# Scaling the weights of a Strassen-like FFN before they are split, and a third accumulator bank

## The chip, the cores and the metric

The kernel runs on one core of one Trainium2 chip. The metric is the device time of one execution in microseconds (us), the median of several runs. The core has a matmul engine (TensorE, PE in the profile, with its weight loads shown apart as PEld), and VectorE (DVE), ScalarE (ACT), GpSimd (POOL) and SyncE (SP, which here only issues transfers). Every engine takes its own queue of instructions strictly in order; semaphores tie the queues to each other.

## The reference

A transformer block on a sequence of 1024 tokens of width 1024: a first FFN, a mixer with two attentions, a second FFN, a final norm. What matters here are the two FFNs:

```
h = rmsnorm(x, ffn_norm)            # (x * rsqrt(mean(x^2) + eps)) * gain
x = x + 0.5 * ((silu(h @ w1) * (h @ w3)) @ w2)     # w1, w3: 1024 x 2816; w2: 2816 x 1024
```

All inputs are fp32. The changed code is the up-projection, `h @ w1` and `h @ w3`, of both FFNs.

## The kernel before

Activations are held transposed: eight tiles of 128 features by 512 tokens for each half of the tokens (tb 0 and 1). The 2816 columns of w1 and w3 are 22 groups f of 128; one weight tile in DRAM, `w13[f, j]`, holds half j of the 1024 rows for one group, w1 and w3 side by side (128 x 1024 values, 512 KB).

*Precision.* A product in fp32 accuracy is made from halves: a tile is split into a high and a low part, and three matmuls (high·high, high·low, low·high) are added up in a PSUM bank. In the first two pairs of groups of an FFN ("plain" blocks, `NPLAIN = 2`) the halves are fp32r. In the other nine pairs (fp = 2 to 10) they are fp16, and to fit the range of fp16 weights and activations are first multiplied by a power of two: `hs` for the activations (from the norm's gains), and one scale per block for the weights. `find_scale` (L342) takes it from the sums of squares of the block's four raw weight tiles: four ACT squares (L340), a matmul with ones that adds them over the partitions (L344, output `tot`), then seven small DVE instructions (L346, L102 to L111). The second output, `inv`, undoes both scales and is applied where PSUM is read.

`split16` (L93 to L95) makes the fp16 halves: ACT writes `scale * src` as fp16, and DVE writes `scale * src - high` as fp16, with a scalar_tensor_tensor. `form` (L317) does this for one weight tile into the next of eight slots.

*A block.* Instead of eight products of 2 x 2 sub-blocks a block of two column groups takes seven (a Strassen-Winograd scheme). The raw tiles are a11, a21, a22, a12; four sums of them are made in place or in `s1`, `s4` (L425 to L428), by POOL, in the first block by DVE:

```
se.tensor_tensor(out=s1, in0=a21, in1=a22, op=ALU.add)          # L425: S1
se.tensor_tensor(out=a21, in0=a11, in1=a21, op=ALU.subtract)    # L426: S3
se.tensor_tensor(out=a11, in0=s1, in1=a11, op=ALU.subtract)     # L427: S2
se.tensor_tensor(out=s4, in0=a12, in1=a11, op=ALU.subtract)     # L428: S4
```

The activations' sub-blocks B11, B21, B22 and sums T1 to T4 are split once, ahead of the blocks (`scale_h`, `right_sums`). Each product is 24 matmuls (two banks m = 0, 1 for w1 and w3, four tiles, three terms), all on line L397. In the order of the code they are: A11·B11 into X (`first_product`, written at the end of the block before, right after that block's `find_scale` call for the next block); S2·T2 into Y; S1·T1 into Z; A12·B21 on top of X; S3·T3 on top of Y; then, after the next block's scale and its A11·B11, A22·T4 on top of Y and S4·B22 into Z. Between them the partial sums are read: ACT copies X after A11·B11 (L407, `s`), DVE adds Y and `s` after S2, S3 and A22 (L433: outputs u for S2 and S3, c for A22), adds Z (L455 after S1, L469 after S4), and L442, L443 finish the first output. SiLU and the gate follow (L510 on ACT, L511 on POOL), and the results and four sums of them (L479, POOL) go to DRAM for the down-projection. Between, DVE also makes sums of the w2 tiles (L499 to L505) for it.

X, Y and Z have two PSUM banks each, and the same two in every block. One bank is for `tot`; one of the eight is not used. Raw tiles are double-buffered, so the next block's tiles are loaded and squared during a block.

*What sets the order.* The code is not run in the order in which it is written. A planner fixes each engine's queue before the run: it goes through an assumed timeline, and gives each engine the earliest written instruction whose inputs it takes to be ready at that moment. An instruction can thus be put ahead of earlier written ones that still wait. At run time the queues are not changed any more. A few instructions are moved by a priority offset (`high_priority`) or a fixed order (`order_after`).

Of the kernel before, what the change touches and what calls it, by code (L numbers as in the profile page):

```python
# [7 lines left out]
F32 = mybir.dt.float32  # L8
# [4 lines left out]
AF = mybir.ActivationFunctionType  # L13
ALU = mybir.AluOpType
# [4 lines left out]
P = 128  # L19
T = 1024  # L20
TB = 512
# [3 lines left out]
KD = 8  # L25
# [64 lines left out]
    return lo_of(nc, lo, src, hi)  # L90


def split16(nc, t, src, scale):  # L93
    nc.scalar.activation(out=t[:, 0], in_=src, func=AF.Copy, scale=scale)  # L94
    return nc.vector.scalar_tensor_tensor(out=t[:, 1], in0=src, scalar=scale, in1=t[:, 0], op0=ALU.mult, op1=ALU.subtract)  # L95


def pow2_scale(K, pool, tot, shift, other=None):
# [16 lines left out]
def gain_scales(K, pool):  # L115
    nc = K.nc
    sq = pool.tile([P, 4, KD], F32, tag="gsq", name="gsq")
    nc.vector.tensor_tensor(out=sq, in0=K.gain, in1=K.gain, op=ALU.mult)
    r = pool.tile([P, 4], F32, tag="gr", name="gr")
    nc.vector.tensor_reduce(out=r, in_=sq, axis=AX.X, op=ALU.add)  # L120
    tot = K.pt.tile([P, TB], F32, tag="acc", name="tot")[:, 0:4]
    nc.tensor.matmul(tot, lhsT=K.ones, rhs=r, start=True, stop=True)
    K.hs, K.hinv = pow2_scale(K, pool, tot, 57)


def load_w(K, src):
# [110 lines left out]
def scale_h(K, tb, gi, gates=None):  # L237
    nc = K.nc
    K.h[tb], last = [None] * KD, []
    hs = K.hs[:, gi:gi + 1]  # L240
    for k in [i // 2 + i % 2 * (KD // 2) for i in range(KD)] if gates else range(KD):
        x = K.x[tb][k]
        g = K.gain[:, gi, k:k + 1]
        if gates:
            order_after(K, nc.scalar.activation(out=x, in_=x, func=AF.Copy, scale=g), gates[k])
            nc.gpsimd.tensor_tensor(out=x, in0=x, in1=K.R[tb], op=ALU.mult)
        else:
            nc.vector.scalar_tensor_tensor(out=x, in0=x, scalar=g, in1=K.R[tb], op0=ALU.mult, op1=ALU.mult)
        if gates:
            K.h[0][k] = K.hp.tile([P, 2, TB], F16, tag=f"hi0_{k}", name="h16")  # L250
            split16(nc, K.h[0][k], x, hs)
            continue
        hi = K.hp.tile([P, TB], F32R, tag=f"hi{tb}_{k}", name="hi")
        lo = K.hp.tile([P, TB], F32R, tag=f"lo{tb}_{k}", name="lo")
        last.append(split(nc, hi, lo, x))
        K.h[tb][k] = hi, lo
    if gates:
        K.b22 = []
        for k in range(KD // 2):
            K.b22.append(K.hp.tile([P, 2, TB], F16, tag=f"lo0_{k}", name="h16"))  # L260
            split16(nc, K.b22[k], K.x[1][k + KD // 2], hs)
    return last


# [6 lines left out]
    return x  # L271


def right_sums(K, tp, gi):
    nc = K.nc
    h = KD // 2
    T = [[], [], [], []]

    def put(i, k, src):
        t = (tp if i else K.hp).tile([P, 2, TB], F16, tag=f"t{i}_{k}" if i else f"lo0_{k + h}", name="tf")  # L280
        split16(nc, t, src, K.hs[:, gi:gi + 1])
        T[i].append(t)
    for k in range(h):
        b11, b21, b12, b22 = K.x[0][k], K.x[0][k + h], K.x[1][k], K.x[1][k + h]
        nc.vector.tensor_tensor(out=b11, in0=b12, in1=b11, op=ALU.subtract)
        put(0, k, b11)
        nc.gpsimd.tensor_tensor(out=b12, in0=b22, in1=b12, op=ALU.subtract)
        put(2, k, b12)
        nc.vector.tensor_tensor(out=b22, in0=b22, in1=b11, op=ALU.subtract)
        put(1, k, b22)  # L290
        nc.gpsimd.tensor_tensor(out=b21, in0=b21, in1=b22, op=ALU.subtract)
        put(3, k, b21)
    return T

# [14 lines left out]
def ffn_up(K, w13, w2, ctx0, gi, first):  # L309
    nc = K.nc  # L310
    h = KD // 2
    ctx = ExitStack()
# [1 line left out]
    bank = lambda n, m: ps.tile([P, TB], F32, tag=f"{n}{m}", name=n)  # L314
    K.nw = 0

    def form(src, sc):  # L317
        n = len(K.wpools)
        t = K.wpools[K.nw % n].tile([P, 2, KD, P], F16, tag=("whi", "wlo")[K.nw // n % 2], name="w16")
        K.nw += 1  # L320
        split16(nc, t.rearrange("p a k c -> p a (k c)"), src.rearrange("p k c -> p (k c)"), sc)
        return t

    def store(f, tb, t):
# [24 lines left out]
    with ExitStack() as c1:  # L349
# [5 lines left out]
        r = load(NPLAIN)  # L355
        nu = 0
        for tb, p in ((0, 0), (0, 1), (1, 1), (1, 0)):
            for f in range(2):
                nu += 1
                u = [bank("XYZ"[nu % 3], m) for m in range(2)]  # L360
                for m in range(2):
                    for k in range(KD):
                        mm3(nc, u[m], ws[p][2 * f + k // h], m * h + k % h, K.h[tb][k], k == 0, k == KD - 1)
                t = sb.tile([P, TB], F32, tag="s", name="s")
                if tb == 0:
                    nc.vector.tensor_tensor(out=t, in0=u[0], in1=K.R[0], op=ALU.mult)
                    order_after(K, nc.scalar.activation(out=t, in_=t, func=AF.Silu), K.rdone)
                    nc.gpsimd.tensor_tensor(out=t, in0=t, in1=K.R[0], op=ALU.mult)
                else:
                    nc.scalar.activation(out=t, in_=u[0], func=AF.Silu)  # L370
                nc.vector.tensor_tensor(out=t, in0=u[1], in1=t, op=ALU.mult)
                store(2 * p + f, tb, t)
            if (tb, p) == (0, 0):
                gates = scale_h(K, 1, gi)
            if (tb, p) == (0, 1):
                scale_h(K, 0, gi, gates)
                for i in range(4):
                    square(r, i)
                scale, inv = find_scale(r, K.pt)
    K.nw = 0  # L380
    T = right_sums(K, open_pool(K, ctx, "tf", 1, side="right"), gi)
    ctx0.close()
    with ctx:
        pt = open_pool(K, ctx, "up_tot", 1, True)
        sums = open_pool(K, ctx, "up_sums", 1)
        rw.append(open_pool(K, ctx, "up_raw2", 1))
        po = open_pool(K, ctx, "up_post", 1)
# [9 lines left out]
                    K.mark = nc.tensor.matmul(o, lhsT=w[:, a, m * h + k], rhs=x[k][:, b], start=start and k == 0 and i == 0,  # L397
                                              stop=k == h - 1 and i == 2, skip_group_check=True)

        def first_product(a11, sc, inv):  # L400
            X = [bank("X", m) for m in range(2)]
            w = form(a11, sc)
            s = []
            for m in range(2):
                prod(X[m], w, m, B11, True)
# [2 lines left out]
            return X, s  # L408

        n0, n1 = NPLAIN, NF // 2  # L410
        X, sv = first_product(r[0][0], scale, inv)
        for fp in range(n0, n1):
            f0, f1 = 2 * fp, 2 * fp + 1
            a11, a21, a22, a12 = r[0]
# [4 lines left out]
            for n in ("u2", "u3", "c21", "c11"):  # L419
                for m in range(2):  # L420
                    if n != "c11" or m == 0:
                        u[n, m] = po.tile([P, TB], F32, tag=f"{n}{m}", name=n)
            Y, Z = [[bank(n, m) for m in range(2)] for n in "YZ"]
            se = nc.vector if fp == n0 else nc.gpsimd
            se.tensor_tensor(out=s1, in0=a21, in1=a22, op=ALU.add)  # L425
            se.tensor_tensor(out=a21, in0=a11, in1=a21, op=ALU.subtract)  # L426
            se.tensor_tensor(out=a11, in0=s1, in1=a11, op=ALU.subtract)  # L427
            se.tensor_tensor(out=s4, in0=a12, in1=a11, op=ALU.subtract)  # L428
            ws2, ws1, wa12, ws3 = [form(t, scale) for t in (a11, s1, a12, a21)]

            def add(n, o, i, inv):
                for m in range(2):
# [21 lines left out]
            for m in range(2):  # L454
                nc.vector.scalar_tensor_tensor(out=u["u3", m], in0=Z[m], scalar=inv, in1=u["u3", m], op0=ALU.mult, op1=ALU.add)  # L455
            finish_a(K, u["u3", 0], u["u3", 1], f1, 1, store)
            wa22, ws4 = form(a22, scale), form(s4, scale)
            old = inv
            if fp + 1 < n1:
                scale, inv = find_scale(r, pt)  # L460
                X, nxt = first_product(r[0][0], scale, inv)
            for m in range(2):
                prod(Y[m], wa22, m, T[3], False)
            add("c21", Y, sv, old)
# [1177 lines left out]
```

## Time and profile before

| | us |
|---|---|
| median of 3 runs | 2987.51 (2986.30 to 2988.24) |
| the profiled execution | 2990.17 |
| its span, first to last instruction | 2988.4 |
| seven-product blocks of FFN 1, about | 104 to 467 |
| seven-product blocks of FFN 2, about | 2403 to 2761 |

The granted TensorE clock is 0.986 of full speed. In a row of the profile `L95 DVE SCALAR_TENSOR_TENSOR w<-a,sc,w` is line 95, the engine, the operation, the output and the inputs by their names in the code; durations follow in ns or, in a timeline, start and length in us; a bracket `[0.82 <-DVE w L95]` is the engine's idle time ahead of the instruction and what ended it. In a wait table, `PE Y L397 <- DVE u L433: 29.0, 15, 3.2` says that PE waited 29.0 us in 15 places, 3.2 at the longest, with a matmul into Y, for line 433 on DVE. A stretch's row gives its length and then each engine's busy time and number of instructions.

### The profile page before, as it was taken

How to read it: one execution, taken by the hardware profiler on the slowest of the kernel's cores; microseconds unless marked ns; L12 is line 12 of the kernel's file. 1: busy time of each engine (PE TensorE's matmuls, PEld its weight loads, DVE VectorE, ACT ScalarE, POOL GpSimd, SP SyncE). 2: the span in 40 equal slices, each digit the busy share in tenths (PEclk: the TensorE clock that was granted, in tenths of full speed). 3: DMA queues.
4: the chain of work that ended last, by engine and by line, in shares of the span. 5: the costliest groups of instructions: out<-in, count | busy, mean ns of one | idle time of the engine just before them, and what ended most of it. 6: DMA issues, size and time to landing. Idle time of an engine off the chain costs nothing. (4 is left out here: it accounts for less than half of the span.)

```text
span 2988.4 us, 40209 instructions
## 1 busy us (share of the span) xinstructions
PE 2835.6 (95%) x14276; PEld 2128.7 (71%) x14276; DVE 1995.5 (67%) x3282; ACT 1370.2 (46%) x2347; POOL 951.9 (32%) x765
## 2 busy tenths in 40 slices
PE   8998999999999899989899999999999998999998
PEld 6543447888788688778788888888878853444886
DVE  7866566666587467667777777776333966665656
ACT  7434334443333145445566666666432644432443
POOL 3348441000145123322333333333242436554101
PEclk9999999999999999999999999999999999999999
DMA  4354447655456544544332235222743246444854
GB/s 159 117 194 170 178 155 267 214 189 163 147 200 230 184 142 169 186 157 163 127 117 86 82 115 161 79 83 77 289 152 109 77 149 208 173 151 157 298 183 148
DMA packets 212712, 478.21 MB, mean 160 GB/s; under 512 B 20896, under 2 KB 39584, under 8 KB 212512
## 3 DMA queue, kind: packets, MB, share of 16 engines
q1 hardware_dynamic: 212512, 475.65, 46.2%
q8 instruction: 112, 1.84, 0.3%
q14 instruction: 88, 0.72, 0.1%
HBM read 313.56 MB, written 162.00 MB: 159 GB/s over the span
## 5 line engine op out<-in xcount | busy, mean ns | idle before, releaser
L397 PEld LDWEIGHTS <-w 128*128 128x128 f16 x3024 | 298.4, 99 | 414.4 <-issue 45.9
L52 PE MATMUL gm<-hi,whi 128*128 128x512 f32 x880 | 352.1, 400 | 3.3 <-ACT whi L89 1.9
L397 PE MATMUL Y<-tf,w 128*128 128x512 f16 x1296 | 304.2, 389 | 48.0 <-DVE u L433 29.0
L54 PE MATMUL gm<-hi,wlo 128*128 128x512 f32 x880 | 348.4, 397 | 0.3 <-DVE wlo L85 0.3
L53 PE MATMUL gm<-lo,whi 128*128 128x512 f32 x880 | 348.3, 396 | 0.0
L861 PE MATMUL S<-kt,qt 128*128 128x320 f32 (+5 forms) x1152 | 274.9, 352 | 36.4 <-ACT Pt L870 12.2
L85 DVE TENSOR_TENSOR tl<-tr,th 128x512 fp32r<-128x512 f32 (+2 forms) x384 | 236.2, 619 | 88.3 <-ACT th L89 85.0
L89 ACT ACTIVATE th<-tr 128x512 fp32r<-128x512 f32 (+2 forms) x384 | 203.8, 542 | 198.2 <-PE tr L916 194.7
L85 DVE TENSOR_TENSOR wlo<-st,whi 128x1024 fp32r<-128x1024 f32 x154 | 197.4, 1299 | 112.6 <-ACT whi L89 111.5
L868 DVE CUSTOM_DVE_ANT_0 S<-S,slab 128x896 f32<-128x896 f32 (+7 forms) x320 | 224.4, 708 | 65.5 <-PE S L861 59.5
L53 PE MATMUL acc<-wlo,whi 128*128 128x512 f32 (+1 forms) x628 | 243.1, 387 | 1.0 <-DVE wlo L85 1.0
L54 PE MATMUL acc<-whi,wlo 128*128 128x512 f32 (+1 forms) x628 | 242.1, 388 | 0.0
L89 ACT ACTIVATE whi<-st 128x1024 fp32r<-128x1024 f32 x154 | 160.6, 1057 | 177.2 <-PE acc L54 107.4
L52 PE MATMUL acc<-whi 128*128 128x512 f32 (+1 forms) x628 | 240.4, 387 | 0.0
L1027 POOL TENSOR_SCALAR Ps<-Ps,l 128x384 f32<-128x384 f32 (+7 forms) x128 | 100.8, 787 | 425.0 <-DVE l L1025 216.4
L861 PEld LDWEIGHTS S<-kt,qt 128*128 128x128 f32 x1152 | 183.4, 190 | 61.0 <-ACT Pt L870 14.2
L397 PE MATMUL X<-h,w 128*128 128x512 f16 x864 | 195.1, 379 | 0.0
L52 PEld LDWEIGHTS gm<-hi,whi 128*128 128x128 f32 x880 | 168.5, 191 | 36.3 <-ACT whi L89 2.1
L54 PEld LDWEIGHTS gm<-hi,wlo 128*128 128x128 f32 x880 | 168.1, 191 | 36.8 <-DVE wlo L85 0.9
L95 DVE SCALAR_TENSOR_TENSOR w<-a,sc,w 128x1024 f16<-128x1024 f32 x90 | 180.3, 2019 | 18.8 <-ACT w L94 17.4
L53 PEld LDWEIGHTS gm<-lo,whi 128*128 128x128 f32 x880 | 168.6, 192 | 30.8
L85 DVE TENSOR_TENSOR wlo<-wst,whi 128x1024 fp32r<-128x1024 f32 x103 | 137.0, 1332 | 44.1 <-ACT whi L89 32.9
(320 smaller groups left out, 6260.8 us busy)
## 6 DMA issues: line engine op xcount, KB each, us to landing
wst<-in_win_dram SPq DMA_DIRECT2D x55, 512.0 KB
sw<-w2s SPq DMA_DIRECT2D x44, 512.0 KB
st<-sw SPq DMA_DIRECT2D x88, 256.0 KB
st<-saT SPq DMA_DIRECT2D x88, 256.0 KB
a<-in_f1w_dram SPq DMA_DIRECT2D x36, 512.0 KB
a<-in_f2w_dram SPq DMA_DIRECT2D x36, 512.0 KB
st<-saB SPq DMA_DIRECT2D x66, 256.0 KB
qt<-sq SPq DMA_DIRECT2D x128, 128.0 KB
```

The costliest lines, as they stand in the source:

```text
L52: first = nc.tensor.matmul(out, lhsT=w[0][:, wk], rhs=x[0], start=start, stop=False, skip_group_check=skip)
L53: nc.tensor.matmul(out, lhsT=w[0][:, wk], rhs=x[1], start=False, stop=False, skip_group_check=skip)
L54: nc.tensor.matmul(out, lhsT=w[1][:, wk], rhs=x[0], start=False, stop=stop, skip_group_check=skip)
L85: return nc.vector.tensor_tensor(out=lo, in0=src, in1=hi.bitcast(F32), op=ALU.subtract)
L89: nc.scalar.activation(out=hi, in_=src, func=AF.Copy)
L95: return nc.vector.scalar_tensor_tensor(out=t[:, 1], in0=src, scalar=scale, in1=t[:, 0], op0=ALU.mult, op1=ALU.subtract)
L397: K.mark = nc.tensor.matmul(o, lhsT=w[:, a, m * h + k], rhs=x[k][:, b], start=start and k == 0 and i == 0, stop=k == h - 1 and i == 2, ski ...
L861: K.last = nc.tensor.matmul(S[:, o:o + n], lhsT=q, rhs=k[:, k0 + c:k0 + c + n], start=i == 0, stop=i == 1)
L868: nc.vector.tensor_tensor_reduce(out=sv, in0=sv, in1=mv, scale=-0.125, scalar=BIG, op0=ALU.add, op1=ALU.min, accum_out=nm)
L1027: nc.gpsimd.tensor_scalar(out=p[:, 0:n], in0=p[:, 0:n], scalar1=l[:, c:c + 1], scalar2=1.0, op0=ALU.mult, op1=ALU.mult)
```

## The change

Three things. First, `split16` has no scale any more: ACT makes a plain copy to fp16, DVE a plain subtract (tensor_tensor). The weights' scale is applied by ACT to the four raw tiles in place (`prescale`), in `first_product`, once the block's scale is known: a11, then A11's split, then a21, a22, a12. The sums are thus made from scaled tiles. Second, the activations' power of two is multiplied into the gains of the norm once (`K.gs`), so that x itself is scaled; the plain products of the second half of the tokens, which read that x, undo it by `K.hinv` (in SiLU's scale operand and a scalar_tensor_tensor). Third, Y's two banks are taken in turn from three, one block after the other; the third is in a pool of its own.

```
-def split16(nc, t, src, scale):
-    nc.scalar.activation(out=t[:, 0], in_=src, func=AF.Copy, scale=scale)
-    return nc.vector.scalar_tensor_tensor(out=t[:, 1], in0=src, scalar=scale, in1=t[:, 0], op0=ALU.mult, op1=ALU.subtract)
+def split16(nc, t, src):
+    nc.scalar.activation(out=t[:, 0], in_=src, func=AF.Copy)
+    return nc.vector.tensor_tensor(out=t[:, 1], in0=src, in1=t[:, 0], op=ALU.subtract)
...
-    K.hs, K.hinv = pow2_scale(K, pool, tot, 57)
+    hs, K.hinv = pow2_scale(K, pool, tot, 57)
+    K.gs = pool.tile([P, 4, KD], F32, tag="gs", name="gs")
+    nc.vector.tensor_tensor(out=K.gs, in0=K.gain, in1=hs.unsqueeze(2).broadcast_to([P, 4, KD]), op=ALU.mult)
...
-        g = K.gain[:, gi, k:k + 1]
+        g = K.gs[:, gi, k:k + 1]
...
-                    nc.scalar.activation(out=t, in_=u[0], func=AF.Silu)
-                nc.vector.tensor_tensor(out=t, in0=u[1], in1=t, op=ALU.mult)
+                    nc.scalar.activation(out=t, in_=u[0], func=AF.Silu, scale=K.hinv[:, gi:gi + 1])
+                if tb == 0:
+                    nc.vector.tensor_tensor(out=t, in0=u[1], in1=t, op=ALU.mult)
+                else:
+                    nc.vector.scalar_tensor_tensor(out=t, in0=u[1], scalar=K.hinv[:, gi:gi + 1], in1=t,
+                                                   op0=ALU.mult, op1=ALU.mult)
...
+        p3 = open_pool(K, ctx, "up_y", 1, True)
...
-        def first_product(a11, sc, inv):
+        def prescale(t, sc):
+            nc.scalar.activation(out=t, in_=t, func=AF.Copy, scale=sc)
+
+        def first_product(r, sc, inv):
             X = [bank("X", m) for m in range(2)]
-            w = form(a11, sc)
+            prescale(r[0][0], sc)
+            w = form(r[0][0])
+            for t in r[0][1:]:
+                prescale(t, sc)
...
-            Y, Z = [[bank(n, m) for m in range(2)] for n in "YZ"]
+            Z = [bank("Z", m) for m in range(2)]
+            Y = [ps.tile([P, TB], F32, tag=f"Y{b}", name="Y") if b < 2 else p3.tile([P, TB], F32, tag="Y2", name="Y")
+                 for b in ((2 * (fp - n0) + m) % 3 for m in range(2))]
...
-            ws2, ws1, wa12, ws3 = [form(t, scale) for t in (a11, s1, a12, a21)]
+            ws2, ws1, wa12, ws3 = [form(t) for t in (a11, s1, a12, a21)]
...
-            wa22, ws4 = form(a22, scale), form(s4, scale)
+            wa22, ws4 = form(a22), form(s4)
...
-                X, nxt = first_product(r[0][0], scale, inv)
+                X, nxt = first_product(r, scale, inv)
```

More of the change, by code (lines that the diff above doesn't have):

```diff
@@ L239, in scale_h @@
     K.h[tb], last = [None] * KD, []
-    hs = K.hs[:, gi:gi + 1]
     for k in [i // 2 + i % 2 * (KD // 2) for i in range(KD)] if gates else range(KD):
         x = K.x[tb][k]
-        g = K.gain[:, gi, k:k + 1]
+        g = K.gs[:, gi, k:k + 1]
         if gates:
@@ L250, in scale_h @@
             K.h[0][k] = K.hp.tile([P, 2, TB], F16, tag=f"hi0_{k}", name="h16")
-            split16(nc, K.h[0][k], x, hs)
+            split16(nc, K.h[0][k], x)
             continue
@@ L260, in scale_h @@
             K.b22.append(K.hp.tile([P, 2, TB], F16, tag=f"lo0_{k}", name="h16"))
-            split16(nc, K.b22[k], K.x[1][k + KD // 2], hs)
+            split16(nc, K.b22[k], K.x[1][k + KD // 2])
     return last
@@ L271, in x_tiles, with right_sums @@
     return x
-def right_sums(K, tp, gi):
+def right_sums(K, tp):
     nc = K.nc
@@ L280, in put @@
         t = (tp if i else K.hp).tile([P, 2, TB], F16, tag=f"t{i}_{k}" if i else f"lo0_{k + h}", name="tf")
-        split16(nc, t, src, K.hs[:, gi:gi + 1])
+        split16(nc, t, src)
         T[i].append(t)
@@ L315, in ffn_up, with form @@
     K.nw = 0
-    def form(src, sc):
+    def form(src):
         n = len(K.wpools)
@@ L320, in form @@
         K.nw += 1
-        split16(nc, t.rearrange("p a k c -> p a (k c)"), src.rearrange("p k c -> p (k c)"), sc)
+        split16(nc, t.rearrange("p a k c -> p a (k c)"), src.rearrange("p k c -> p (k c)"))
         return t
@@ L380, in ffn_up @@
     K.nw = 0
-    T = right_sums(K, open_pool(K, ctx, "tf", 1, side="right"), gi)
+    T = right_sums(K, open_pool(K, ctx, "tf", 1, side="right"))
     ctx0.close()
@@ L410, in ffn_up @@
         n0, n1 = NPLAIN, NF // 2
-        X, sv = first_product(r[0][0], scale, inv)
+        X, sv = first_product(r, scale, inv)
         for fp in range(n0, n1):
```

## The prediction

> **What bounds the kernel now.** I read the page's busy shares first, then the two stretches in which the changed products run, then who TensorE waited for.
>
> ```profile
> PE 2835.6 (95%) x14276; PEld 2128.7 (71%) x14276; DVE 1995.5 (67%) x3282; ACT 1370.2 (46%) x2347; POOL 951.9 (32%) x765
> 104.00:467.00 363.00, 337.21 (x1534) 152.00 (x1533) 236.88 (x265) 135.82 (x181) 185.72 (x98) 0.98 0.48 167
> 2403.00:2761.00 358.00, 335.65 (x1536) 151.93 (x1535) 229.98 (x262) 130.17 (x172) 183.67 (x99) 0.99 0.48 169
> ```
>
> TensorE (PE) sets the time: 95% of the span. The nine seven-product blocks of FFN 1 take 363.0 us and those of FFN 2 358.0 us; in them PE is busy 337.2 and 335.7, VectorE (DVE) 237, ScalarE (ACT) 136, GpSimd (POOL) 186. So ACT is free for 227 us of each stretch, and only PE's gaps can be won or lost. The waits of PE over the whole span, in us, times, longest:
>
> ```profile
> PE Y L397 <- DVE u L433: 29.0, 15, 3.2
> PE Y L397 <- DVE w L95: 10.3, 11, 2.1
> PE Y L397 <- DVE c L433: 8.7, 4, 2.2
> ```
>
> The 29.0 lie inside a block: product S3·T3 and then A22·T4 go into the same Y banks, and DVE's add (L433) must read a bank in between. The other 19.0 lie on the seam between two blocks, where S2·T2 of the next block starts. One seam in the timeline (start, length, engine, line):
>
> ```profile
> 333.88 0.28 PE L344 MATMUL tot<-ss,ones 128*128 128x4 f32 x2
> 337.64 0.15 DVE L106 TENSOR_SCALAR sc<-sa 128x1 f32<-128x1 f32 x1
> 337.82 1.15 ACT L94 ACTIVATE w<-a,sc 128x1024 f16<-128x1024 f32 x1 [1.39 <-DVE sc L106]
> 338.88 1.13 ACT L94 ACTIVATE w<-s,sc 128x1024 f16<-128x1024 f32 x1
> 340.37 3.33 POOL L427 TENSOR_TENSOR a<-s,a 128x1024 f32<-128x1024 f32 x1 [1.81 <-DVE w L95]
> 343.73 2.19 ACT L94 ACTIVATE w<-a,sc 128x1024 f16<-128x1024 f32 x2 [1.12 <-POOL a L427]
> 346.96 3.32 POOL L425 TENSOR_TENSOR s<-a,a 128x1024 f32<-128x1024 f32 x1
> 348.66 2.70 DVE L95 SCALAR_TENSOR_TENSOR w<-a,sc,w 128x1024 f16<-128x1024 f32 x1
> 350.52 0.59 PE L397 MATMUL Y<-tf,w 128*128 128x512 f16 x2
> 351.42 4.92 PE L397 MATMUL Y<-tf,w 128*128 128x512 f16 x22 [0.30 <-DVE w L95]
> 352.60 1.25 ACT L407 ACTIVATE s<-X,si 128x512 f32<-128x512 f32 x2
> 356.18 5.34 PE L397 MATMUL Z<-tf,w 128*128 128x512 f16 x24
> 356.79 0.74 DVE L469 SCALAR_TENSOR_TENSOR u<-Z,si,u 128x512 f32<-128x512 f32 x1
> 359.19 1.06 ACT L340 ACTIVATE jk<-a 128x1024 bf16<-128x1024 f32 x1
> 361.36 5.34 PE L397 MATMUL X<-h,w 128*128 128x512 f16 x24
> 371.72 0.28 PE L344 MATMUL tot<-ss,ones 128*128 128x4 f32 x2
> ```
>
> The matmul of the totals (333.88) gives the scale 3.9 us later; with it ACT and DVE make the high and low halves of all weights of the next block in one burst. PE has 72 matmuls (A22·T4, S4·B22, the next A11·B11) that don't hang on this burst beyond its first tile; they last until 350.52, 16.6 us after the totals. Then S2·T2 is next, and its low half comes from the DVE instruction that ends at 351.36. Two things to see: the sum L427 that S2 needs starts right in the burst, because L425 and L426 have been done a block before (the L425 at 346.96 is for the block whose totals run at 371.72); and PE was held 0.30 us only. The costliest kind of seam:
>
> ```profile
> 186.12 0.59 PE L397 MATMUL Y<-tf,w 128*128 128x512 f16 x2
> 188.10 0.73 DVE L433 SCALAR_TENSOR_TENSOR c<-Y,si,s 128x512 f32<-128x512 f32 x1
> 188.77 1.27 DVE L95 SCALAR_TENSOR_TENSOR w<-a,sc,w 128x1024 f16<-128x1024 f32 x1
> 188.90 0.38 PE L397 MATMUL Y<-tf,w 128*128 128x512 f16 x1 [2.18 <-DVE c L433]
> 190.09 6.01 PE L397 MATMUL Y<-tf,w 128*128 128x512 f16 x21 [0.82 <-DVE w L95]
> ```
>
> Here one matmul waits for its Y bank (2.18), but the next one waits until 190.04 for the low half, which stands behind the same L433 in DVE's queue. And after the hole 21 matmuls take 6.01, where 22 took 4.92 above: 1.3 us lost to a slow restart.
>
> **The change part by part.** Prices by line (min/median/max ns), and two rows of the first block, where DVE does the sums:
>
> ```profile
> L94 ACT ACTIVATE w<-a,sc x90: 1132/1135/1152, 93.1 to 2720.9; 128x1024 f16<-128x1024 f32 x90
> L95 DVE SCALAR_TENSOR_TENSOR w<-a,sc,w x90: 1267/1624/3418, 100.8 to 2729.8; 128x1024 f16<-128x1024 f32 x90
> L425 POOL TENSOR_TENSOR s<-a,a x8: 2724/3322/3342, 107.6 to 385.7; 128x1024 f32<-128x1024 f32 x8
> L427 POOL TENSOR_TENSOR a<-s,a x8: 2349/2823/3338, 137.3 to 424.1; 128x1024 f32<-128x1024 f32 x8
> 99.69 1.21 DVE L425 TENSOR_TENSOR s<-a,a 128x1024 f32<-128x1024 f32 x1
> 116.31 0.68 DVE L371 TENSOR_TENSOR s<-Z,s 128x512 f32<-128x512 f32 x1
> 127.34 0.75 DVE L443 SCALAR_TENSOR_TENSOR c<-X,si,c 128x512 f32<-128x512 f32 x1 [0.57 <-PE X L397]
> ```
>
> *Low halves by a plain subtract.* 126 weight tiles go from L95's form (1.27 undisturbed) to that of L425 on DVE (1.21): 0.06 each, 7.6 us of DVE time. DVE has 126 us free in a stretch, so this shortens only the burst, by 7 x 0.06 = 0.4 us; I count 0 (between 0 and 16 x 0.4 = 6.4 gained). That the length of an undisturbed one is not the trouble shows in the median, 1.62, and the maximum, 3.42: DVE and POOL take turns on these tiles (a POOL sum is 2.35 alone and 3.33 with a DVE split put in). The new form reads two SBUF tiles as well, so I let the turns stand. The 56 splits of x and its sums lie ahead of the stretches, in time that PE fills with plain products: 0. The opposite step, the plain blocks' product becoming a scalar form, is 0.75 for 0.68 on 8 instructions, 0.6 us of DVE in the same cover; if it were bare, 0.6 lost.
>
> *Folding the norm scale.* One product of 32 numbers per partition at the start, in place of the scale operand; beside the first loads, 0.
>
> *Four in-place scalings a block.* 72 new ACT instructions of about 1.14 (L94 reads the same tile and scale), 82 us in all, in the 227 us that ACT has free per stretch. What they cost is not ACT's time but place in the burst. For the seam at 333.88: start-to-start on ACT is 1.06 (337.82 to 338.88), so scale a11, form A11, scale a21 and a22 end at 337.82 + 4 x 1.06 = 342.1. A11's halves come 1.06 later; 48 other matmuls (10.4 us; 24 take 5.18, from 356.18 to 361.36) cover that, 0; bare it would cost 16 x 1.06 = 17. But now L425 and L426 read scaled tiles and can no longer run a block ahead: L425, L426, L427 stand in the burst one after another, 3 x 2.35 to 3 x 3.33 = 7.1 to 10.0, so L427 ends at 349.2 to 352.1, where it ended at 343.7. After it S2 needs its form on ACT (1.06) and DVE (1.21), with or without one POOL sum in front of DVE (3.33): ready at 351.5 to 357.7, against 351.36. So S2 is 0.1 to 6.3 us later at each of the 16 seams, 3.2 in the middle. Queued behind: S4 (L428), needed only at the block's end; the loads that wait for these raw tiles to come free, whose squares run up to 360.3 (L340) and whose totals are two blocks off, at the earliest after 371.72: 11 us of slack against 6.3.
>
> *Who takes the hole.* The order on every queue is fixed by the planner, which puts the earliest written instruction that it takes to be ready. It sees the longer chain. Two products of the next block do not need L426 and L427: S1·T1 (L425 alone) into Z, and A12·B21 (no sum at all, a scaled tile and its halves) into X. Each covers 24 matmuls, 5.2 us; 10.4 together, more than 6.3. I take it that one of them is put ahead of S2 at most seams. Then the seams' present price is what can be won, since the first product there hangs on an early instruction of DVE's burst and no longer on its fifth or sixth. That price is 10.3 + 8.7 of waits and four restarts of 1.3: 24.2 us. From both sides: all of it, -24.2; or nothing, because L407's copies (X) and L469's adds (Z), which free those banks, stand in the same late queues (352.60 and 356.79, 2 and 6 us after PE wants to go on at 350.52). I take the middle, -12.
>
> *Third Y bank.* The row at 190.09 says that the bank is not what ends last; alone it is worth 0 (at most the 8.7, which is in the sum above). With the product moved it lets S2 start in a free bank, which is part of why I don't take less than half.
>
> Sum against the profiled execution: 2990.2 (span 2988.4 and 1.8 around it) - 12 = 2978. The median of the runs lies 2.7 below that execution: **2975 us**.
>
> [...]
>
> **The rivals.** *The chain decides (slower).* The planner takes the sums for shorter than they are, leaves S2·T2 first on the seam, and PE, which takes its queue in order, stands at it with A12 and S1 ready behind. For it: at this seam and the one at 186 PE was already sent to S2 before its low half was there, so the planner is too hopeful in the burst. Against: the new chain has two more sums and three more scalings, too much to overlook. It decides from the point where S2 is over 1.5 us later than now (the present 24.2 over 16). Price: 3.2 x 16 = 51 if at all seams, 3039; with half of the seams filled 26, 3013. I put it at 3015.
>
> *No change.* The third bank does nothing, as above; PE's seam gap closes, but with S1 and A12 gone ahead, S3 follows S2 in the same Y banks, and DVE's add stands between them, as between S3 and A22 now: 29.0 over 15 times, 1.9 each. Six such new waits, 11.4, eat the 12: 2987. For it: DVE's queue is behind in just that stretch. Against: if only one product moves, the other lies between.
>
> *All seams close.* 2990.2 - 24.2 - 6.4 (shorter burst) - 2.7 = 2957; little speaks for all at once.
>
> **How the numbers follow.** Gain at the seams 0.45 (2975, own range 2957 to 2981; the full gain is its lower end), no change 0.20, chain 0.35, of which 0.12 with nearly all seams open (over 3024). A measurement here tells about 0.2% (6 us) from nothing. Faster 0.45, same 0.20, slower 0.35. The range: from 2957 (0.05 below it) to 3024 (0.12 above).
>
> **What would show it.** Right: between the totals and the next S2·T2 PE runs more than 72 matmuls, with Z or X of the next block among them; the waits on w L95 and c L433 fall from 19.0 towards 7; L425 and L426 start after the scale; the in-place scalings are 72 at about 1.1; the stretches shrink by some 6 us each; nothing changes outside them. Wrong: S2·T2 still comes after 72 and waits 3 us or more; or the waits on u L433 grow past 29 by what the seams gave; or the two stretches keep their length and the change is elsewhere, since a new plan may also move work after them.

## The result and the profile after

The change makes the kernel slower: 3012.18 us median (3010.40 to 3015.97) against 2986.91 of the kernel before on the same chip, ratio 1.0087, 95% interval 1.0069 to 1.0104. The forecast was 2975 and faster. The time lies in the range, 3 us from the number that the prediction gave to its slower rival, but not by that rival's mechanism.

In the code after, the products are L403 (before L397), the totals L345 (L344), the adds of Y L447 (L433), the product that finishes c L457 (L443), the sums S1, S3, S2, S4 L439 to L442 (L425 to L428), the w2 sums L517 (L503); the in-place scalings are L407. The experiments' kernels have a few lines more or less, so one step can have another number there. The page's busy line of the kernel after, then its stretches (start:end, length, and busy time and instructions of PE, PEld, DVE, ACT, POOL; then clock, DMA share, GB/s):

```profile
PE 2847.3 (95%) x14276; PEld 2131.8 (71%) x14276; DVE 1997.3 (66%) x3283; ACT 1427.9 (47%) x2419; POOL 966.1 (32%) x765
104.00:473.00 369.00, 339.31 (x1530) 151.29 (x1527) 236.44 (x263) 159.57 (x208) 192.97 (x98) 0.97 0.47 163
473.00:2413.00 1940.00, 1860.00 (x9862) 1578.02 (x9861) 1289.37 (x2481) 940.13 (x1781) 517.94 (x525) 0.99 0.45 152
2413.00:2782.00 369.00, 337.16 (x1529) 150.88 (x1527) 235.23 (x262) 159.01 (x205) 192.65 (x98) 0.98 0.47 163
```

The profiled execution took 3013.16, its span 3011.3, 22.9 more than before. The blocks of FFN 1 now take 369.0 (363.0 before), those of FFN 2 369.0 (358.0): 17 of the 22.9. In these two stretches PE is idle for 61.5 us, where it was for 48.1, and busy for 3.6 more. The stretch between, 1940, was 1936 before (467 to 2403); this and the 2 us behind the second stretch are not explained. So most of the loss is where the change is. ACT has 57.7 us more work in all, 47% of the span in place of 46%; DVE is as busy as before. No other engine has become the bound; what PE waits for has changed. Whom PE waited for in the products, kernel after:

```profile
PE X L403 <- DVE w L95: 19.3, 4, 5.0
PE X L403 <- DVE c L457: 18.1, 8, 3.5
PE Y L403 <- DVE u L447: 12.7, 9, 1.8
PE Y L403 <- DVE w L95: 8.2, 4, 2.7
```

In Y the waits fell, as forecast and more: 10.3 + 8.7 at the seam became 8.2, and 29.0 on u became 12.7. But X, for which no wait is listed before, now costs 37.4. The sum of these rows is 58.3; the three rows before made 48.0.

One seam of the kernel after in the timeline:

```profile
300.71 0.15 DVE L106 TENSOR_SCALAR sc<-sa 128x1 f32<-128x1 f32 x1
300.90 4.27 ACT L407 ACTIVATE a<-a,sc 128x1024 f32<-128x1024 f32 x4 [1.39 <-DVE sc L106]
304.20 2.36 POOL L439 TENSOR_TENSOR s<-a,a 128x1024 f32<-128x1024 f32 x1 [2.56 <-ACT a L407]
305.07 0.61 ACT L524 ACTIVATE c<-c 128x512 f32<-128x512 f32 x1
305.59 1.99 ACT L94 ACTIVATE w<-a 128x1024 f16<-128x1024 f32 x2
305.73 5.59 DVE L517 TENSOR_TENSOR w2s<-w2s 128x512 f32<-128x512 f32 x4 [3.77 <-DMA w2s<-in_f1w_dram]
308.42 0.28 PE L345 MATMUL tot<-ss,ones 128*128 128x4 f32 x2
308.56 1.02 PE L403 MATMUL X<-h,w 128*128 128x512 f16 x4
312.56 3.04 DVE L95 TENSOR_TENSOR w<-a,w 128x1024 f16<-128x1024 f32 x2
314.53 7.22 PE L403 MATMUL X<-h,w 128*128 128x512 f16 x20 [4.94 <-DVE w L95]
```

Read it from the scale (300.71). ACT does all four scalings, one silu, and only then A11's high half (305.59). DVE, which had nothing of A11 to do, has stood 3.77 us for the loads of the w2 sums and then goes into them (305.73); the four take 5.59 us beside POOL's sums, and after two more short adds the low half follows at 312.56. All four scalings come ahead of A11's high half at each of the eight seams of FFN 1. PE reaches the low half's first matmul at 309.6 and stands until 314.53. The same tile in the kernel before, counted from the scale at 337.64:

```profile
339.01 1.28 DVE L95 SCALAR_TENSOR_TENSOR w<-a,sc,w 128x1024 f16<-128x1024 f32 x1
```

There the low half was done at 340.29, 2.5 us after the scale was; here at about 314.5, 13.6 us after. The forecast had put it 1.06 later. Second, the totals of the next block (308.42) are planned 7.7 us after this block's scale: the planner now takes the totals of two blocks one shortly after the other at every second seam (before, once in each FFN, at 246.27 and 254.60 in the first), and A11·B11 of a block may follow so early that X's bank is not read yet (the 18.1).

### The profile page after: what moved, and what is told of

It reads as the page before. It is cut to its first block, busy times and chain, and to the rows that moved or that the text cites. A ratio compares the mean times of both kernels' runs of the same rounds, so it can differ in the third digit from the quotient of the medians.

```text
span 3011.3 us, 40228 instructions
## 1 busy us (share of the span) xinstructions
PE 2847.3 (95%) x14276; PEld 2131.8 (71%) x14276; DVE 1997.3 (66%) x3283; ACT 1427.9 (47%) x2419; POOL 966.1 (32%) x765
## 5 line engine op out<-in xcount | busy, mean ns | idle before, releaser
L403 PEld LDWEIGHTS <-w 128*128 128x128 f16 x3024 | 298.5, 100 | 434.0 <-issue 59.4
L403 PE MATMUL Y<-tf,w 128*128 128x512 f16 x1296 | 293.6, 381 | 20.9 <-DVE u L447 12.7
L403 PE MATMUL X<-h,w 128*128 128x512 f16 x864 | 210.1, 399 | 38.1 <-DVE w L95 19.3
L95 DVE TENSOR_TENSOR w<-a,w 128x1024 f16<-128x1024 f32 x90 | 177.5, 1991 | 25.4 <-ACT w L94 25.0
```

The lines of the kernel that those rows point to most:

```text
L95: return nc.vector.tensor_tensor(out=t[:, 1], in0=src, in1=t[:, 0], op=ALU.subtract)
```

## The experiments

All times are medians; each ratio is to the kernel before, run beside it (2985.2 to 2987.3 in all groups), with its 95% interval.

### The parts one by one

The kernel before, with nothing but the third bank for Y:

```
+        p3 = open_pool(K, ctx, "up_y", 1, True)
-            Y, Z = [[bank(n, m) for m in range(2)] for n in "YZ"]
+            Z = [bank("Z", m) for m in range(2)]
+            Y = [... three banks in turn, as in the change ...]
```

> The kernel before with only the third Y bank added; everything else as before. My step (the bank is not what ends last, the low half behind it in VectorE's queue is): within 3 us of before, 2984 to 2990, with the 8.7 us of waits on c L433 passing over to the low half (w L95). Rival, the bank wait counts by itself: 8.7 us less, about 2978.

2986.7, ratio 0.9997 (0.9988 to 1.0007). Its waits in Y:

```profile
PE Y L398 <- DVE u L436: 29.5, 14, 3.2
PE Y L398 <- DVE w L95: 18.6, 9, 3.2
```

Of the three rows of the kernel before the one of 8.7 us on c is gone from the head of the list, and the 10.3 on the low half have become 18.6: nearly the same 19 us under the other name. The bank was not what ended last.

The kernel before, with nothing but the norm's power of two folded into the gains (x's splits without a scale, weights as before):

```
-        g = K.gain[:, gi, k:k + 1]
+        g = K.gs[:, gi, k:k + 1]
-            split16(nc, K.h[0][k], x, hs)
+            split16(nc, K.h[0][k], x)
```

> Only the norm scale folded into the gains, and the splits of x and its sums without a scale; weights split with the scale as before, two Y banks. My step (0, in the cover of the plain products): within 3 us of before. Rival, the loss sits in the plain blocks or in what follows them: up to 3 us slower; a gain of the shorter splits: up to 3 us faster.

2987.43, ratio 1.0003 (0.9993 to 1.0012): nothing.

The kernel after, with Y in two banks as before:

```
-            Y = [... three banks in turn ...]
+            Y, Z = [[bank(n, m) for m in range(2)] for n in "YZ"]
```

> The changed kernel with Y back in its two banks. If the loss comes from the in-place scaling, it stays: 3008 to 3018. If the third bank let the planner choose an order that costs the time, it goes: about 2990.

3011.63, ratio 1.0078 (1.0062 to 1.0095): the loss stays. As the fold is worth nothing either, the loss comes from what is left, the scaling in place with the plain splits of the weights; these two were not run apart.

### Is it the pairing of the totals?

The kernel after, each block's totals held behind the last product of S3:

```
+        first = nc.tensor.matmul(tot, lhsT=K.ones, rhs=r[1], start=True, stop=True)
+        if pt is not K.pt:
+            order_after(K, first, K.mark)
```

> The changed kernel, in which each block's matmul of the totals may not run before S3.T3 of the block before it, as mostly in the kernel before; nothing is left out. The trace of the changed kernel shows the totals of two blocks taken one after the other at every second seam, and A11.B11 of the later block then put right behind S3.T3, where it waits for X's bank (18.1 us on c L457, 8 times). Theory A (that pairing costs): these waits go, 18 us and some restarts, 3012 to about 2990. Theory B (A11's own halves are late behind four scalings on ScalarE; 19.3 us on w L95 in 4 places): pinning puts A11 behind its own scale at all 16 seams instead of 8, the 18 go but up to 8 new waits of 4.9 come, 39: 3012 to 3035.

3049.96, ratio 1.0208 (1.0193 to 1.0223), above both ranges. Theory A is out: without the pairing the time is 38 us worse. Its waits:

```profile
PE Y L405 <- DVE u L449: 48.2, 19, 6.3
PE X L405 <- DVE w L95: 34.4, 12, 5.1
```

The waits on c in X are gone, but with one set of totals per seam A11's low half is late twelve times instead of four. This speaks for A11's halves as the trouble, as in theory B; the 48.2 on u (12.7 before) were in neither theory.

### A11's place in the two queues

The kernel after, the other three scalings behind A11's high half on ACT:

```
             for t in r[0][1:]:
-                prescale(t, sc)
+                order_after(K, prescale(t, sc), K.high)
```

> The kernel after, but ScalarE scales S's other three raw tiles only behind A11's high half. Theory B (A11's halves are late because the three other scalings stand ahead of its high half): the high half is written some 3.4 us sooner (three scalings of 1.04 to 1.15), VectorE can take A11's low half ahead of the w2 sums, and the four waits of 4.9 us on A11's low half go with their restarts of about 2.7: 3012 - 4 x 7.6 = about 2982, at least below 2995. Rival C (VectorE is held by the w2 sums, whose operands come by DMA, and takes them first whatever ScalarE does): the waits on A11's low half stay at 4 us or more, 3005 to 3015.

3014.83, ratio 1.0091 (1.0071 to 1.0112): the time is in C's range, but C's mechanism is not what is seen. The wait on A11's low half did go (2.8 of 19.3 are left), as B said, so the scalings in front of it are part of its cause; but the time did not move. Other rows took its place:

```profile
PE X L403 <- DVE c L457: 24.4, 8, 4.9
PE Y L403 <- DVE u L447: 16.0, 6, 3.1
PE Z L403 <- DVE w L95: 8.7, 5, 2.1
```

The same with the totals held as well:

> As the one before (three scalings behind A11's high half), and each block's totals also held behind the last product of S3, which cost 37 us in the kernel after (3050 against 3012). Theory B: the pinned seams were dear because A11's halves came late at each of them, so most of it goes: 2975 to 2995. Rival C (VectorE takes the w2 sums first): 3035 to 3050. Rival D (the pairing of two blocks' totals was a gain by itself): 3000 to 3020.

3028.86, ratio 1.0143 (1.0117 to 1.0169): 21 below the pinned run without it, and between the expectations. X's wait on the low half is 3.7 there (34.4 without the edit); u in Y, 54.1, is left.

The kernel after, A11's halves cut from the raw tile with the scale in the instruction, as before, and the four tiles scaled afterwards:

```
-            prescale(r[0][0], sc)
-            w = form(r[0][0])
-            for t in r[0][1:]:
+            w = form(r[0][0], sc)
+            for t in r[0]:
                 prescale(t, sc)
```

> The kernel after, but A11's two halves are taken straight from the raw tile with the scale in the instruction, as in the kernel before, and all four raw tiles are scaled in place only then. Theory B: A11's halves come as early as before, S2 comes later, and Z or X of the next block stands ahead of it, which is my forecast's own mechanism: 2970 to 2980, and no wait of over 2 us on A11's low half. Rival D (the later S2 costs more than the planner can fill): 2995 to 3015. Rival C: as after, 3005 to 3015.

3012.54, ratio 1.0085 (1.0061 to 1.0109): what "C" and "D" said, and no gain, though PE waits no more on A11's halves and the planner puts Z and X of the next block ahead of S2·T2 at most seams. Its waits:

```profile
PE Y L406 <- DVE u L449: 30.5, 13, 7.2
PE Z L406 <- DVE w L96: 16.9, 6, 3.6
```

and one of the longest in its timeline:

```profile
250.71 0.75 DVE L449 SCALAR_TENSOR_TENSOR u<-Y,si,s 128x512 f32<-128x512 f32 x1 [6.00 <-DMA saT<-u]
251.51 6.79 PE L406 MATMUL Y<-tf,w 128*128 128x512 f16 x18 [6.07 <-DVE u L449]
```

DVE stood at u's sum because the u tile was still being stored for the block before (`saT`), and PE stood at the Y bank that this sum reads. Moreover S1's low half, which S1·T1 in Z needs, is late too: the product that was to fill the hole hangs on the same queue.

### DVE and the w2 sums

The kernel after, and then the kernel before, without the four additions of each w2 sum. What they compute is another result, since the down-projection then multiplies other weights; they only serve to show what the additions cost:

```
-    for out, a, b, op in ((a22, a21, a22, ALU.add), ...):
-        nc.vector.tensor_tensor(out=out, in0=a, in1=b, op=op)
```

> The kernel after with the four VectorE additions of each w2 sum left out: w2's tiles are loaded and stored without them, so the third stage multiplies other weights. 64 additions, most of them between the totals of a block and A11's low half. Rival C (VectorE held by the w2 sums): the waits on A11's low half fall below 1 us, 2975 to 2990. Theory B (ScalarE's order): they fall only by the part that the sums add, 3.5 of 4.9 at most, and the time stays at 2995 to 3005.

> The kernel before with the four VectorE additions of each w2 sum left out: w2's tiles are loaded and stored without them, so the third stage multiplies other weights. It is the partner of the kernel after without them (2988). Theory C (VectorE, held by w2 sums that wait for their loads, makes u's sums and A11's halves late): TensorE's 29.0 us of waits on u go, with some 10 to 20 of restarts: 2940 to 2960, and the change without w2 sums then costs still 30 to 45. Rival F (the w2 sums hurt only the kernel after, through A11's place on ScalarE): 2980 to 2988, and the change without them costs nothing.

After without them 2987.98 (ratio 1.0000, 0.9990 to 1.0010); before without them 2954.40 (0.9894, 0.9879 to 0.9909). The sums cost the kernel after 24 us and the kernel before 32. In the kernel after the wait on A11's low half in X is gone without them, so they are part of its cause too, beside the scalings; the 22.2 on c in X stay. In the kernel before the waits on u fall from 29.0 to 14.8. So the sums are dear in both, and they do not explain the difference: without them the change still costs 33.6.

Next they stay in, but their additions are held behind A11's low half of the next block, and their loads are released by the same product as before (all jobs of that list are also written later, behind the next block's first product):

```
-            for job in jobs[done[0]:done[1]]:
-                job()
+            K.w2mark = K.mark
...
                 X, nxt = first_product(...)
+            for job in jobs[done[0]:done[1]]:
+                job()
...
-        nc.vector.tensor_tensor(out=out, in0=a, in1=b, op=op)
+        order_after(K, nc.vector.tensor_tensor(out=out, in0=a, in1=b, op=op), K.a11low)
```

In the kernel before:

> The kernel before with the w2 sums' additions held behind A11's low half of the next block on VectorE; their loads are released by the same product as before. Theory C: the 29.0 us of waits on u fall below 10, S2's halves may come a little later for the additions that now stand between: 2955 to 2972. Rival G (the additions are only moved into the chain that S2 waits for): 2980 to 3000, with more wait on S2's low half than 10.3.

2972.09, ratio 0.9951 (0.9933 to 0.9969). As theory C said: the row on u in Y leaves the list of waits (3.1 us of 29.0 are left), while the low half of S2 and c cost 15.4 + 13.5 in place of 19.0. A faster kernel by moving one job.

In the kernel after:

> The kernel after with the w2 sums' additions held behind A11's low half of the next block on VectorE. Theory C: the four waits of 4.9 us on A11's low half go with their restarts, and the waits of 12.7 on u fall; the 18.1 on c stay: 2970 to 2985. Theory B (ScalarE's order alone): the waits on A11's low half stay over 3 us, 3000 to 3012.

3039.40, ratio 1.0177 (1.0162 to 1.0192): a miss for both. The waits on A11's low half are gone; in their place PE waits 33.5 us on u in Y and, 8 times at the seams with paired totals, 25.1 more in Y (the list names L104; beside it a low half ends, at 244.70). DVE in one such seam:

```profile
239.67 0.14 DVE L102 TENSOR_SCALAR sa<-one 128x1 f32<-128x1 f32 x1
239.73 2.77 DVE L520 TENSOR_TENSOR w2s<-w2s 128x512 f32<-128x512 f32 x1
242.42 2.28 DVE L95 TENSOR_TENSOR w<-a,w 128x1024 f16<-128x1024 f32 x1
244.63 0.14 DVE L104 TENSOR_SCALAR sa<-sa 128x1 int32<-128x1 int32 x1
...
250.71 0.14 DVE L106 TENSOR_SCALAR sc<-sa 128x1 f32<-128x1 f32 x1
```

The second block's scale is a chain of instructions of 0.14 us each, and the planner has strewn it between w2 sums and halves that take 2 to 3 us: from L102 to L106 it needs 11.2 us, where the seam of the kernel after shown above needs 0.7 (300.16 to 300.86). How much of the 27 us above the kernel after this makes is not shown.

In the kernel with A11's halves from the raw tile:

> The kernel with A11's halves straight from the raw tile and the four scalings behind them (3012.5), and the w2 sums' additions held behind A11's low half. Theory C: its 30.5 us of waits on u fall below 12; the 16.9 on S1's low half in Z stay or grow: 2975 to 2990. If the w2 sums only change places, 3005 to 3015.

2987.18, ratio 1.0004 (0.9995 to 1.0014), 25 below the run without the move. Against the same kernel without the scaling (2972.09) the change costs 15 here.

### The store that sets u2 free

One edit, two buffers in place of one for u2, in four kernels:

```
-                        u[n, m] = po.tile([P, TB], F32, tag=f"{n}{m}", name=n)
+                        u[n, m] = (po2 if n == "u2" else po).tile([P, TB], F32, tag=f"{n}{m}", name=n)
```

> The kernel before with two buffers in place of one for u2. Theory H (VectorE waits with u2's sum until the stores of the block before have read u2's tile, 102 us of idle time ahead of that line, and holds Y's banks and what is queued behind it): the 29.0 us of waits on u in Y fall below 12: 2960 to 2975. If u2's sum only waits while nothing needs it: 2983 to 2990.

> The kernel after with two buffers in place of one for u2. Theory H (the scaling moves S's sums on GpSimd into the burst at the seam, ahead of the sums of the block before whose stores set u2's tile free; VectorE stands at u2's sum and the product of c, which frees X, stands behind it): the 18.1 us of waits on c in X and the 12.7 on u go, the 19.3 on A11's low half stay: 2985 to 2998. Theory I (the weights' halves come late by ScalarE and GpSimd alone): 3008 to 3015.

> The kernel before with the w2 sums' additions behind A11's low half (2972) and two buffers for u2: 2955 to 2970 if the two gains add; 2970 to 2975 if the later additions had already taken the wait on u2.

> The changed kernel with A11's halves from the raw tile, the w2 sums' additions behind A11's low half (2987) and two buffers for u2. It differs from the one without in-place scaling (the run beside it) by the change alone. Theory H: the change's loss was u2's release, so it stands within 6 of that run, 2955 to 2975. Theory I (S1's and S2's halves wait for ScalarE's scalings and GpSimd's sums, a chain of its own): the 19.1 us of waits on S1's low half in Z stay, 12 or more above that run, 2970 to 2990.

Before: 2980.92 (0.9980, 0.9970 to 0.9989), a small gain between the two expectations. DVE's group of that line, in the kernel with two buffers (busy, mean, idle time ahead of it and what ended it):

```profile
L433 DVE SCALAR_TENSOR_TENSOR u<-Y,si,s 128x512 f32<-128x512 f32 x72 | 52.0, 741 | 19.4 <-PE Y L397 11.5 <-ACT s L407 4.7 <-DMA saT<-u 3.2
```

and in the kernel before:

```profile
L433 DVE SCALAR_TENSOR_TENSOR u<-Y,si,s 128x512 f32<-128x512 f32 x72 | 53.5, 746 | 123.5 <-DMA saT<-u 101.8 <-POOL u L479 8.6 <-PE Y L397 7.4
```

102 us of DVE's standing at that store fell to 3, and PE's wait on u only from 29.0 to 21.4: DVE then stands at the w2 loads, 119.7 us in place of 75.9. After: 3012.34 (1.0092, 1.0075 to 1.0109), nothing, as theory I had it. With the w2 sums later and no scaling: 2974.56 (0.9961, 0.9946 to 0.9976), no further gain. With the later sums, A11 from the raw tile and the scaling: 2970.72 (0.9945, 0.9929 to 0.9960). This last one differs from the one at 2974.56 by the change (A11's halves apart), and the change costs nothing there, in time as theory H had it. Nor does it gain what it was forecast to: the waits of 15.4 on S2's low half and 13.8 on c in Y have become

```profile
PE Z L407 <- DVE w L96: 27.3, 14, 2.0
PE Y L407 <- DVE w L96: 5.4, 7, 0.8
```

The hole moved from S2·T2 to S1·T1, which was put ahead to fill it (theory I's wait, without its price).

### One part taken back

From the last kernel, first with Y in two banks again (the edit as above):

> The run with A11 from the raw tile, later w2 sums and two buffers for u2 (2970.7), with Y in two banks again. Where the seams are closed the third bank may count at last: 2975 to 2985 with waits on u or c in Y. If it is worth nothing even here: 2968 to 2974.

2968.40, ratio 0.9946 (0.9929 to 0.9963): the third bank is worth nothing here either. Then, with three banks, A11's halves cut from the scaled tile, as in the change. This kernel also holds each block's totals behind S3's last product; in the one beside it they stand there by themselves at all 16 seams, so that the place of the totals in PE's queue is the same in both:

```
-            w = form(r[0][0], sc)
-            for t in r[0]:
+            prescale(r[0][0], sc)
+            w = form(r[0][0])
+            for t in r[0][1:]:
                 prescale(t, sc)
...
+        if pt is not K.pt:
+            order_after(K, first, K.mark)
```

> The run with A11 from the raw tile, later w2 sums and two buffers for u2 (2970.7), with one part taken back: A11 is scaled in place with the other three first and its halves are cut from the scaled tile, as in the changed kernel; the totals are held behind S3's last product, where that run has them by itself. Theory B (the disputed term: A11's halves come late behind the scalings, and at every seam TensorE runs out of work ahead of them): 16 seams of 2 to 3, or over 3000: 3000 to 3030. My forecast's own step (48 matmuls cover the delay, 0): 2968 to 2976.

3038.53, ratio 1.0177 (1.0162 to 1.0192): 68 us more, 4.2 for each of the 16 seams and above the range of theory B, for a delay that the forecast had as 1.06 and covered. A seam with A11 from the raw tile (2970.72):

```profile
287.22 0.15 DVE L109 TENSOR_SCALAR sc<-sa 128x1 f32<-128x1 f32 x1
287.41 1.15 ACT L97 ACTIVATE w<-a,sc 128x1024 f16<-128x1024 f32 x1 [2.54 <-DVE sc L109]
288.59 1.28 DVE L98 SCALAR_TENSOR_TENSOR w<-a,sc,w 128x1024 f16<-128x1024 f32 x1
307.66 1.22 DVE L96 TENSOR_TENSOR w<-a,w 128x1024 f16<-128x1024 f32 x1
308.94 1.25 PE L407 MATMUL Y<-tf,w 128*128 128x512 f16 x5 [0.83 <-DVE w L96]
```

and one with A11 from the scaled tile (3038.53):

```profile
351.91 0.15 DVE L106 TENSOR_SCALAR sc<-sa 128x1 f32<-128x1 f32 x1
352.10 4.27 ACT L410 ACTIVATE a<-a,sc 128x1024 f32<-128x1024 f32 x4 [1.39 <-DVE sc L106]
356.79 1.99 ACT L94 ACTIVATE w<-a 128x1024 f16<-128x1024 f32 x2
358.12 3.17 DVE L95 TENSOR_TENSOR w<-a,w 128x1024 f16<-128x1024 f32 x1
367.44 3.41 PE L406 MATMUL Z<-tf,w 128*128 128x512 f16 x15 [1.17 <-DVE w L95]
373.53 2.28 DVE L95 TENSOR_TENSOR w<-a,w 128x1024 f16<-128x1024 f32 x1
375.87 6.16 PE L406 MATMUL Y<-tf,w 128*128 128x512 f16 x20 [3.08 <-DVE w L95]
```

From the scale to the end of A11's low half: 2.5 us (287.37 to 289.87) and 9.2 (352.06 to 361.29). PE waits only 0.71 for A11 itself. But DVE starts its burst of seven low halves 4.8 us later and ends the first 6.7 later, and what stands behind is late in turn: S2's low half comes 21.5 us after the scale in the one and 23.8 in the other, and PE stands 1.17 at Z and 3.08 at Y. The scale itself comes 2.5 us later after the totals in the second, behind adds of u and a w2 sum on DVE; so not all of the difference is A11's own delay. Over the whole kernel PE's waits on low halves are 43.0 in Y, 15.4 in Z and 4.1 in X; with 13.3 on u and 6.6 on high halves that is 82, where the kernel beside it waits 34. Most of the rest of the 68 are slow matmuls after the holes: 20 take 6.16 behind the 3.08, where 20 take 4.48 elsewhere, and the matmuls into Y together take 312.1 us for 293.4.

## Why the prediction was wrong, point by point

*What bounds the kernel.* Right: PE at 95% of the span, and most of what changes is PE's gaps in the two stretches. One row was read too narrowly: the 29.0 us of waits on u do not all lie between S3·T3 and A22·T4. In the timeline six of the 15, 14.5 us, stand ahead of S3·T3, for u2's sum after S2·T2, as here, where the totals and S3 follow A12·B21:

```profile
249.42 5.34 PE L397 MATMUL Y<-tf,w 128*128 128x512 f16 x24 [2.88 <-DVE u L433]
```

So the new wait that the second rival feared between S2 and S3 was there before the change already, with S1 and A12 between the two, and u2's sum is the one that stands at the store.

*Third bank, 0 alone.* Right, in three surroundings (2986.7 beside 2987.3; 3011.6 beside 3012.2; 2970.7 beside 2968.4). The reading behind it, that the low half stands behind the same add, is what its row shows: 8.7 + 10.3 became 18.6.

*Fold of the norm's scale, 0.* Right.

*Low halves by plain subtract, 0 counted.* The price of one was right. Rows of the kernel after:

```profile
L95 DVE TENSOR_TENSOR w<-a,w x90: 1206/1272/3394, 98.9 to 2742.6; 128x1024 f16<-128x1024 f32 x90
L407 ACT ACTIVATE a<-a,sc x72: 1131/1134/1154, 74.3 to 2715.7; 128x1024 f32<-128x1024 f32 x72
```

1206 undisturbed against 1267; the maximum, beside a POOL sum, is still 3.39 (3.42): at 322.88 one takes 3.38 while L442 on POOL, 2.35 at its shortest, takes 3.35 from 321.84 on. The plain subtract was not tried by itself.

*Four in-place scalings.* Their price, 72 at 1.134, was right, and that ACT has room for them too. The step that failed is the one after: "A11's halves come 1.06 later; 48 other matmuls (10.4 us) cover that, 0". Both halves of it were wrong. It took ACT's order from the code (scale a11, form A11, scale the rest). The planner, which does not go by that order alone, put all four scalings first, and in the seam shown a silu behind them; so A11's high half comes 4.7 us later and the low half, which then meets the w2 sums or POOL, 6.7 (in the last pair of runs) to 11.1 (in the seam shown of the kernel after). And the cover was counted for PE alone: 48 matmuls hide A11's own wait (0.71 of it is left in the second seam of the last pair), but six further low halves, the w2 sums and the adds that free the banks are behind A11's in DVE's queue, and DVE does not pass by an instruction that waits: in the kernel at 3012.54 the totals end at 245.44, and the scale's first step, which reads them, runs at 253.01, behind the 6.00 that DVE stands at u's sum. The price bare was put at 17; in the last pair it measured 68. That is the price in that surrounding, where the w2 sums are tied to A11's low half and move with it, and not a share of the 25 us: in the kernel after, taking A11's halves from the raw tile gained nothing by itself.

*Who takes the hole.* The plan was right in part: in the kernel after the planner puts Z of the next block ahead of S2·T2 at the first seam of each pair and leaves S2·T2 first at the second, where it does not wait; in the kernel at 2970.7 it puts Z and part of X ahead. The waits in Y on low halves and on c fell from 19.0 to 8.2, of which 5.4 are S2's. That this would gain 12 was wrong even where nothing else goes amiss (2970.7 beside 2974.6): S1·T1 waits in Z for a low half from the same queue, 27.3 us. The text had late queues (L407, L469) as the reason for its bound of no gain, and then took the middle. Of its signs of being right three came true, the products put ahead, the fall of the waits, and L425 and L426 after the scale, while the time rose: they all look at S2·T2, and the loss came from another place. The sign that failed was the length of the stretches.

*The rivals.* "The chain decides" has the right sign and nearly the right time (3015), but its mechanism did not occur: where S2·T2 is left first it does not wait, and PE waits less for it than before. That its time is near is luck. "No change", by new waits between S2 and S3 in Y, did not occur either: the waits on u in Y fell. What came instead, the late A11 and X's bank, was in no rival. That a hole is followed by slow matmuls, which the prediction counted at 1.3 in the seams' present price, the traces bear out; see the last section.

What the change's loss of 25 is made of in its own surroundings stays partly open. Its largest new wait, on A11's low half, is shown to come from the four scalings and the w2 sums ahead of it, but taking the wait away did not bring the time back. Each single mend there (the others' scaling later, A11 from the raw tile, two buffers for u2, two banks) left the time at 3012 to 3015: other waits grew where one was mended, and each edit made the planner write a new order. What is shown is the joint result: with the w2 sums later, two buffers for u2 and A11 from the raw tile the scaling is free, and without the last of the three it costs 68. That GpSimd's sums, now in the burst, delay the store that sets u2 free was the theory for the second of the three; it agrees with 2987.2 falling to 2970.7, but not with the buffer's doing nothing for the kernel after, so if it holds, it does so only where A11 is out of the way.

The fastest kernels that leave nothing out are those of the last steps, 2968 to 2975, not told apart by these runs; of them the kernel before with its w2 sums later (2972.09, 0.9951) is the smallest edit, and the scaling in place is not needed for it.

## What to carry to other kernels

When a step is moved, take its order from the plan of each queue, not from the code, and price the delay for every instruction behind it on that queue: cover by PE's other work holds for the first of them only (here 0.71 us of waiting for A11 itself at the seam shown, and 68 us in all). Where several queues are late at the same place, one mend alone may show nothing; here it took three together, so a zero from one mend was no proof against its cause. And a product put ahead to fill a hole only helps if its own operands do not come out of the queue that made the hole (S1·T1, put ahead, waited 27.3 us in all).

## What was not expected of the hardware

A hole can cost PE more than its length. Four holes of the kernel after, and what follows them:

```profile
174.70 5.28 PE L403 MATMUL X<-h,w 128*128 128x512 f16 x12 [3.49 <-DVE c L457]
346.71 2.75 PE L403 MATMUL X<-h,w 128*128 128x512 f16 x12 [1.65 <-DVE c L457]
242.71 4.49 PE L403 MATMUL Y<-tf,w 128*128 128x512 f16 x20 [2.72 <-DVE w L95]
2551.97 6.18 PE L403 MATMUL Y<-tf,w 128*128 128x512 f16 x20 [2.71 <-DVE w L95]
```

After 3.49 us the next 12 matmuls take 5.28, after 1.65 they take 2.75. After 2.72 the next 20 take their usual 4.49, and after 2.71, at the same place of the second FFN, 6.18. After the 4.94 at 314.53, 20 took 7.22, and the other three holes of 4.5 to 5 us were followed by 20 in 6.18 to 6.99. So in this kernel a hole of 3 to 5 us cost 1.7 to 2.7 on top, and one of 2.4 to 2.7 nothing or 1.5 to 1.7. The granted clock goes with it: it is 0.50 from 314.53 to about 320, and 1.00 from 320.5 to 346; behind the hole at 242.71 it is 1.00 all through. The prediction counted a restart at 1.3 from one seam of the kernel before; the four seams of that kind there paid 1.3, 1.3, 1.7 and 2.9. So 1.3 was the least of them. In the kernel after, the clock was also at 0.50 after a hole of 2.37 us (from 252.16 to 255), and 10 matmuls took 3.82 there, where 10 take 2.32 at 300.65.
